# Mixture-of-experts output: accumulating scatters into a DRAM copy of the residual, in place of two scattered halves that are added on chip

## The chip, the cores and the metric

One core of a Trainium2 chip runs the whole program once. The metric is the device time of one execution in microseconds (us), given as the median of several runs. A profile is one execution with its instructions and transfers recorded. The engines are named as the profile names them: PE (matrix multiply), PEld (its weight loads), DVE (vector), ACT (scalar), POOL (GpSimd), SP (the engine that issues most transfers).

## The reference, cut to what matters

Two layers over 512 tokens of 1024 float32 values. Layer 0 mixes tokens with a recurrence (RWKV-7), layer 1 with forgetting attention ("fox" in the code). Each mixer is followed by a mixture of 16 experts, two of which each token uses:

```python
for i in range(DEPTH):                       # DEPTH = 2
    h = layer_norm(ALPHA * h + mixed, ln_g[i, 0], ln_b[i, 0])
    ffn = shared_router_moe(h, ...)          # top 2 of 16 experts for each token
    h = layer_norm(ALPHA * h + ffn, ln_g[i, 1], ln_b[i, 1])

# in shared_router_moe: gate = gate / sum(gate) for the two chosen experts, rows sorted by expert,
hid = silu(xb @ w_gate[e]) * (xb @ w_up[e]); ys = hid @ w_down[e]
out = segment_sum(ys * row_gate, row_tok)    # each token gets the sum of its two experts' rows
```

## The kernel before, in words

Tokens lie on 128 partitions, so 512 tokens are four token tiles (0 to 3). Matmuls are done in split precision: every weight and every input is split into a high and a low part (ACT copies the high part, DVE subtracts it), and three products are summed (lines 67 to 70). TensorE therefore runs three matmuls for one.

**Before an expert stage** each token tile is normalised (`ln_steps`), and `After.norm` (line 1300) writes it to the DRAM tensor `hd`: tiles 0 to 2 by POOL's queue, tile 3 by SP's.

**The expert stage** (`moe`) goes through the 16 experts in a fixed order. Weights come in pieces of 1 MB through eight buffers (`raw0` to `raw5`, `rawo0`, `rawo1`); a piece is asked for by SP when DVE has split what lay in its buffer (`wsplitB`). For expert e POOL issues, in this order: the scatter of expert e-1's rows (line 338), the gather of the rows of expert e+2 into `xg` (line 252), and the gather of the rows beyond 128 of expert e+1 into `xo` (line 261). PE turns `xo` in `xposeB` (line 309) near the end of expert e, between the two halves of its last weight piece, whether there are such rows or not. An expert with over 128 rows runs a further block `more(e)`, with a scatter of its own. The rows in one of two buffers `yt` are scattered with

```python
st=nc.gpsimd.indirect_dma_start(out=yd[:,:],out_offset=bass.IndirectOffsetOnAxis(ap=ix[0:n],axis=0),
    in_=y[0:n],in_offset=None,bounds_check=2*T-1,oob_is_err=False)
for o in scat: tc.declare_no_dep(st.ins,o.ins,reason="rows of other slots")
```

into a DRAM tensor `yd` of 1024 rows: row `token` for a token's first expert, row `512 + token` for its second (`dst`). No two scatters share a row, so none waits for another. Unused places in the list of 128 indices are out of bounds and are skipped.

**After the expert stage** `Combine` forms ALPHA*h + y0 + y1 for each token tile and normalises it. The last pieces of `load` bring `hd` back into `raw4` and `raw5` while the last expert runs. When all scatters have landed, SP issues eight loads from `yd` (line 474: y0 and y1 of four tiles). How a tile is summed is chosen by a letter: 'D' on DVE (line 493), 'G' on POOL and DVE (lines 487, 488), 'P' by matmuls with the identity into PSUM (line 482), 'V' partly so and the last addition on DVE (line 490). The layers use 'DVPG' and 'PVPV'. After layer 0, `fox` follows: each tile is normalised (lines 123 to 148), turned on PE (line 1075), split (lines 1076 and 1078), and the value matmuls start (line 68). After layer 1 the tiles are normalised and written out (line 1359). `spread` and `spread2` copy the norm's gain and bias to all partitions by way of PE and ACT.

The order of the work on each engine is written by `Threads.run`: generators give the planner their modelled durations, and it emits the steps in the order of modelled time. `FX_SCHED` holds the start times that it is given for the attention layer: four for the token tiles and one for the split of the value weights are its last numbers that matter here. `th.sooner` decides by the same model whether DVE or POOL does a multiplication or addition of the norm's gain and bias (line 148).

## Time and profile before

| what | value |
|---|---|
| median of 3 runs | 1652.01 us (1647.05 to 1655.39) |
| the profiled execution, its own time | 1651.01 us |
| its span, first to last instruction | 1649.3 us |
| PE / PEld / DVE / ACT / POOL busy | 90% / 73% / 71% / 56% / 31% |
| mean granted TensorE clock | 0.93 |
| transfers | 317.81 MB, 193 GB/s over the span |

The two expert stages lie at about 535 to 887 us and 1257 to 1608 us, the attention layer between them, and the last norm after 1608 us. A busy share is an average over stages with different limits, so the stages are read one by one below. The profiled execution lies 1.0 us under the median of the runs shown.

### The profile page before, as it was taken

To read this page: it belongs to the slowest core of one execution; us is meant where nothing else is said; L and a number is where in the kernel's file an instruction comes from. 1 tells how busy PE (TensorE), PEld (TensorE's weight loads), DVE (VectorE), ACT (ScalarE), POOL (GpSimd) and SP (SyncE) were. 2 spreads that over 40 slices of the span, in tenths; PEclk is the share of its full clock that TensorE was granted. 3 is DMA by queue.
4 is the path that set the end of the run, shared out by engine and by line. 5 is a ranking of instruction groups with operands and counts; after the bars stand their busy time and mean duration, and the time that the engine had idled before them with its cause. 6 is when DMAs were issued, how large, how long until landed. Compare 5 with 4: busy or idle time off the path is not lost. (4 is left out here: it accounts for less than half of the span.)

```text
span 1649.3 us, 25004 instructions
## 1 busy us (share of the span) xinstructions
PE 1485.4 (90%) x9185; PEld 1199.9 (73%) x9185; DVE 1173.0 (71%) x1883; ACT 924.3 (56%) x1359; POOL 519.3 (31%) x423
## 2 busy tenths in 40 slices
PE   6998976988885999999998799999985999999995
PEld 2587865877764788888885677777674888888882
DVE  7647779577685796968995637556647786969874
ACT  2554574534334585858784436545424876858753
POOL 4104775413331442333321422101105332323311
PEclk8989998688996999999998899999996999999997
DMA  7325532133435697988994223112417896969954
GB/s 219 122 83 192 161 101 72 27 100 113 131 119 207 225 360 262 331 299 296 363 321 173 92 72 121 46 51 71 163 68 237 268 365 235 365 232 359 352 179 156
DMA packets 203609, 317.81 MB, mean 193 GB/s; under 512 B 27978, under 2 KB 123554, under 8 KB 203444
## 3 DMA queue, kind: packets, MB, share of 16 engines
q1 hardware_dynamic: 181060, 276.13, 49.3%
q0 software_dynamic: 17664, 33.11, 5.8%
q10 hardware_dynamic: 4720, 6.44, 1.1%
q8 instruction: 94, 1.54, 0.4%
q14 instruction: 71, 0.58, 0.1%
HBM read 304.80 MB, written 37.55 MB: 208 GB/s over the span
## 5 line engine op out<-in xcount | busy, mean ns | idle before, releaser
L202 DVE TENSOR_TENSOR wl<-raw,wh 128x2048 fp32r<-128x2048 f32 (+1 forms) x168 | 334.5, 2005 | 5.6 <-DVEq L345 5.6
L199 ACT ACTIVATE wh<-raw 128x2048 fp32r<-128x2048 f32 (+1 forms) x168 | 282.6, 1688 | 14.1 <-ACT wh L199 8.6
L68 PE MATMUL bank<-wh,xm 128*128 128x256 f32 (+1 forms) x768 | 249.8, 325 | 3.9
L69 PE MATMUL bank<-wl,xm 128*128 128x256 f32 (+1 forms) x768 | 245.1, 319 | 0.0
L70 PE MATMUL bank<-wh,xm 128*128 128x256 f32 (+1 forms) x768 | 245.0, 319 | 0.0
L338 POOL DMA_INDIRECT yd<-yt,TB x38 | 91.4, 2406 | 438.2 <-ACT yt L305 389.7
L68 PEld LDWEIGHTS bank<-wh,xm 128*128 128x128 f32 x768 | 144.6, 188 | 26.1 <-issue 14.6
L69 PEld LDWEIGHTS bank<-wl,xm 128*128 128x128 f32 x768 | 144.7, 188 | 11.4
L70 PEld LDWEIGHTS bank<-wh,xm 128*128 128x128 f32 x768 | 144.5, 188 | 11.4
L202 DVE TENSOR_TENSOR wl<-rawo,wh 128x2048 fp32r<-128x2048 f32 (+1 forms) x56 | 110.2, 1980 | 24.9 <-ACT wh L199 24.4
L68 PE MATMUL bank<-wh,wh 128*128 128x512 f32 x256 | 112.4, 439 | 3.1 <-DVE wl L1078 1.7
L68 PE MATMUL bank<-wh,hm 128*128 128x512 f32 x256 | 111.3, 435 | 0.0
L70 PE MATMUL bank<-wh,wl 128*128 128x512 f32 x256 | 102.2, 399 | 2.6 <-DVE wl L1264 2.6
L69 PE MATMUL bank<-wl,wh 128*128 128x512 f32 x256 | 101.5, 396 | 0.0
L70 PE MATMUL bank<-wh,hm 128*128 128x512 f32 x256 | 101.0, 395 | 0.0
L69 PE MATMUL bank<-wl,hm 128*128 128x512 f32 x256 | 100.8, 394 | 0.0
L199 ACT ACTIVATE wh<-rawo 128x2048 fp32r<-128x2048 f32 (+1 forms) x56 | 93.4, 1669 | 12.8 <-PE bank L70 9.0
L1086 POOL TENSOR_TENSOR wl<-raw,wh 128x512 fp32r<-128x512 f32 x29 | 41.4, 1442 | 86.7 <-ACT wh L1085 86.7
L261 POOL DMA_INDIRECT xo<-hd,TB x30 | 62.2, 2072 | 13.0 <-issue 8.6
L64 ACT ACTIVATE xm<-bank 128x512 fp32r<-128x512 f32 x64 | 38.3, 598 | 46.4 <-PE bank L279 45.3
L68 PEld LDWEIGHTS bank<-wh,wh 128*128 128x128 f32 x256 | 49.4, 193 | 16.4 <-issue 5.7
L1221 ACT ACTIVATE sb<-sb,st 128x512 f32<-128x512 f32 (+1 forms) x64 | 35.7, 559 | 45.7 <-DVE st L1217 29.3
(544 smaller groups left out, 3561.4 us busy)
## 6 DMA issues: line engine op xcount, KB each, us to landing
raw<-in_moe_w_gate_dram SPq DMA_DIRECT2D x48, 1024.0 KB, 8.5
raw<-in_moe_w_up_dram SPq DMA_DIRECT2D x48, 1024.0 KB, 9.9
raw<-in_moe_w_down_dram SPq DMA_DIRECT2D x48, 1024.0 KB, 7.5
rawo<-in_moe_w_up_dram SPq DMA_DIRECT2D x16, 1024.0 KB, 5.5
rawo<-in_moe_w_down_dram SPq DMA_DIRECT2D x16, 1024.0 KB, 7.5
rawo<-in_moe_w_gate_dram SPq DMA_DIRECT2D x14, 1024.0 KB, 8.3
raw<-in_fx_w_in_dram SPq DMA_DIRECT2D x12, 1024.0 KB, 6.3
raw<-in_rw_wk_dram SPq DMA_DIRECT2D x4, 1024.0 KB, 12.5
```

Of the source, the lines that this page charges most:

```text
L64: nc.scalar.activation(hi,src,AF.Copy)
L68: nc.tensor.matmul(out,ah,bh,start=start,stop=False)
L69: nc.tensor.matmul(out,ah,bl,start=False,stop=False)
L70: nc.tensor.matmul(out,al,bh,start=False,stop=stop)
L199: Q=slice(None) if q is None else QS[q]; nc.scalar.activation(his[m%NH][:,Q],raws[m%NR][:,Q],AF.Copy)
L202: Q=slice(None) if q is None else QS[q]; V.tensor_tensor(los[m%NH][:,Q],raws[m%NR][:,Q],his[m%NH][:,Q].bitcast(F32),op=ALU.subtract)
L261: nc.gpsimd.indirect_dma_start(out=xo,out_offset=None,in_=hd.rearrange("t (h n) -> (t h) n",h=2), in_offset=bass.IndirectOffsetOnAxis(ap=T ...
L338: st=nc.gpsimd.indirect_dma_start(out=yd[:,:],out_offset=bass.IndirectOffsetOnAxis(ap=ix[0:n],axis=0), in_=y[0:n],in_offset=None,bounds_ch ...
L1086: (V if d else G).tensor_tensor(lo[n][:,Q],raw[:,Q],hi[n][:,Q].bitcast(F32),op=ALU.subtract)
L1221: S.activation(SB[u][:,0:N],SB[u][:,0:N],AF.Exp,bias=ST[u][:,0:1],scale=-1.0,accum_out=ST[u][:,1:2])
```

## The change

A second DRAM tensor, `zd`, gets a copy of each normalised tile beside `hd` (four more writes for each layer, all by POOL's queue). The expert rows are added into `zd` by the scatter itself (`compute_op=ALU.add`), at row `token` (`src`), for a token's first and second expert alike. The declaration that scatters are independent is gone, so each scatter waits for the one before it to land. The gates are divided by ALPHA, so that `zd` ends as h + ffn/ALPHA, and the norm's epsilon is divided by ALPHA squared. `Combine` loses its letters, its additions, its loads of `hd` and `yd`; it loads four tiles of `zd`. The start times of the attention layer's token tiles go from 2, 5, 8, 11 to 0, 2, 4, 6 and that of the value weights' split from 20 to 15; the last norm's tiles start 2 modelled us apart instead of 3.

```diff
-    nc.vector.tensor_scalar(sm[:,14:15],sm[:,13:14],LN_EPS,None,op0=ALU.add)
+    nc.vector.tensor_scalar(sm[:,14:15],sm[:,13:14],eps,None,op0=ALU.add)
...
-        scat=[]
         def scatter(ix,y,n):
-            st=nc.gpsimd.indirect_dma_start(out=yd[:,:],out_offset=bass.IndirectOffsetOnAxis(ap=ix[0:n],axis=0),
-                in_=y[0:n],in_offset=None,bounds_check=2*T-1,oob_is_err=False)
-            for o in scat: tc.declare_no_dep(st.ins,o.ins,reason="rows of other slots")
-            scat.append(st)
+
+            nc.gpsimd.indirect_dma_start(out=zd[:,:],out_offset=bass.IndirectOffsetOnAxis(ap=ix[0:n],axis=0),
+                in_=y[0:n],in_offset=None,bounds_check=T-1,oob_is_err=False,compute_op=ALU.add)
...
-                scatter(dst(e,1),y,64)
+                scatter(src(e,1),y,64)
...
-            lo(4); dnA(w[5],5,1); outA(1,y,fo); scatter(dst(e),y,128); hi(5); lo(5)
+            lo(4); dnA(w[5],5,1); outA(1,y,fo); scatter(src(e),y,128); hi(5); lo(5)
...
-        V.tensor_tensor(red[:,2,0:4],red[:,1,0:4],red[:,1,4:8],op=ALU.add); V.reciprocal(red[:,2,0:4],red[:,2,0:4])
+        V.tensor_tensor(red[:,2,0:4],red[:,1,0:4],red[:,1,4:8],op=ALU.add); V.reciprocal(red[:,2,0:4],red[:,2,0:4]); V.tensor_scalar(red[:,2,0:4],red[:,2,0:4],1.0/ALPHA,None,op0=ALU.mult)
...
-    def load_h(s, j):
-        s.C.nc.sync.dma_start(s.C.raws[4+j].rearrange("p (i n) -> p i n",i=2),s.hd[j*256:(j+1)*256,:].rearrange("(i p) n -> p i n",p=128))
-    def load_y(s, yd, y1, late):
...
-    def add(s, i, t, **k):
-        for n in range(2): s.C.nc.tensor.matmul(s.C.bk[2*i+n],s.C.ident,t[:,n*512:(n+1)*512],skip_group_check=True,**k)
+    def load_z(s):
+        for i in range(NT): s.C.nc.sync.dma_start(s.h[i],s.zd[i*128:(i+1)*128,:])
...
-        yield from ln_steps(C,th,z,i,s.h[i],s.gb,s.bb)
+        yield from ln_steps(s.C,th,s.h[i],i,s.h[i],s.gb,s.bb,eps=LN_EPS/ALPHA**2)
...
-FX_SCHED=(0,.5,-1,0,2,5,8,11,20)+(0,)*16
+FX_SCHED=(0,.5,-1,0,0,2,4,6,15)+(0,)*16
...
-    comb.load_y(yd,[tp.tile([128,D],F32,name=f"y1{i}") for i in range(NT)],True)
+    comb.load_z(); comb.spread(); comb.spread2()
...
         (s.C.nc.sync if i==NT-1 else s.C.nc.gpsimd).dma_start(s.hd[i*128:(i+1)*128,:],out)
+        s.C.nc.gpsimd.dma_start(s.zd[i*128:(i+1)*128,:],out)
...
-        cb[0].how='DVPG'
...
-        cb[1].how='PVPV'; cb[1].load_y(yd,[part(C.raws[i//2],i%2) for i in range(NT)],False)
+        cb[1].load_z()
         th=Threads()
         def last(i):
-            yield 3.0*i
+            yield 2.0*i
```

What moves is seen in the order of the instructions on an engine. At the start of the attention layer, PE has before the identity matmuls that sum the residual (line 482), then the turns of the tiles (line 1075), each row of which is one bank, and the first value matmul (line 68); `raw4` holds tiles 0 and 1, `raw5` tiles 2 and 3:

```order
L482 MATMUL bank2_3948<-raw4_65,ident_74 128x512 [waits DMAHW1_49,Activation_49]
L482 MATMUL bank3_3949<-raw4_65,ident_74 128x512
L482 MATMUL bank4_3950<-raw5_66,ident_74 128x512 [waits DMAHW2_49,Activation_49]
...
L1075 MATMUL bank0_3946<-ident_74,raw4_65 128x128 [waits DVE_49]
...
L1075 MATMUL bank1_3947<-ident_74,raw4_65 128x128 [waits DVE_49]
...
L1075 MATMUL bank2_3948<-ident_74,raw4_65 128x128 x4
L1075 MATMUL bank4_3950<-ident_74,raw5_66 128x128 [waits Activation_49,Pool_49]
...
L68 MATMUL bank0_3946<-wh0_3931,wh4_3935 128x512 [waits DVE_49]
```

Now the same stretch of PE has no sums, and the turns of six half tiles instead of four stand ahead of the first value matmul:

```order
L1051 MATMUL bank0_3952<-ident_74,raw4_65 128x128 [waits DMAHW1_49,DVE_49]
...
L1051 MATMUL bank1_3953<-ident_74,raw4_65 128x128 [waits Pool_49]
...
L1051 MATMUL bank2_3954<-ident_74,raw4_65 128x128 [waits DMAHW2_49,Pool_49]
...
L1051 MATMUL bank3_3955<-ident_74,raw4_65 128x128 [waits DVE_49]
...
L1051 MATMUL bank4_3956<-ident_74,raw5_66 128x128 [waits DMAHW3_49,DVE_49,Activation_49]
...
L1051 MATMUL bank6_3958<-ident_74,raw5_66 128x128 [waits DMAHW4_49,Activation_49,Pool_49]
...
L68 MATMUL bank0_3952<-wh0_3937,wh4_3941 128x512 [waits Activation_49]
```

The first value matmul has thus moved behind the turns of the first halves of tiles 2 and 3 (`bank4`, `bank6`).

At the very end, DVE before takes the statistics of tile 0 from PSUM (`bank0`, `bank1`) when PE has summed it, and adds for tile 1 (line 490) ahead of its statistics:

```order
L123 BN_STATS sm_90<-bank0_3946 128x6 [waits PE_49]
L123 BN_STATS sm_90<-bank1_3947 128x6 [waits PE_49]
L124 BN_AGGR sm_90<-sm_90 128x2 [waits DVE_49]
...
L148 TENSOR_TENSOR raw4_65<-raw4_65,raw2_63 128x512 [waits DMAHW2_49,DMAHW0_49,Activation_49]
L490 TENSOR_TENSOR raw4_65<-raw0_61,bank2_3948 128x512 [waits DMAHW7_49,PE_49]
L490 TENSOR_TENSOR raw4_65<-raw0_61,bank3_3949 128x512 [waits PE_49]
```

Now its statistics wait for a load alone:

```order
L123 BN_STATS sm_90<-raw4_65 128x6 [waits DMAHW4_49]
L123 BN_STATS sm_90<-raw4_65 128x6
L124 BN_AGGR sm_90<-sm_90 128x2 [waits DVE_49]
...
L123 BN_STATS sm_90<-raw4_65 128x6 [waits DMAHW5_49]
...
L148 TENSOR_TENSOR raw4_65<-raw4_65,raw2_63 128x512 [waits DMAHW3_49,Pool_49]
L123 BN_STATS sm_90<-raw5_66 128x6 [waits DMAHW6_49]
```

PE has left this chain, and no addition stands between the statistics of one tile and the next.

In the expert stage, POOL before issues the two gathers and the scatter of one expert, with `xg` and `xo` the gathered rows and `yt` the rows to be scattered; the scatter waits for ACT, which writes its rows, and for the transfer that last used its buffer:

```order
L338 DMA yd0_3960<-yt1_3971,TB_3962 1024x1024 [waits DMASW0_49,DVE_49]
L345 UNCONDITIONAL_BRANCH
L345 ISA [waits DMASW0_49]
...
L252 DMA xg0_3968<-hd0_135,TB_3962 128x1024 [waits DMASW1_49,PE_49]
L261 DMA xo_3972<-hd0_135,TB2_3963 128x512 [waits DVE_49,DMASW6_49,PE_49,Activation_49]
L338 DMA yd0_3960<-yt0_3970,TB_3962 1024x1024 [waits DMASW3_49,Activation_49]
```

Now:

```order
L339 DMA zd0_137<-yt1_3976,TB_3967 512x1024 [waits DMASW3_49,DVE_49]
L344 UNCONDITIONAL_BRANCH
L344 ISA [waits DMASW4_49]
...
L253 DMA xg0_3973<-hd0_135,TB_3967 128x1024 [waits DMASW5_49,PE_49]
L262 DMA xo_3977<-hd0_135,TB2_3968 128x512 [waits DVE_49,DMASW2_49,PE_49,Activation_49]
L339 DMA zd0_137<-yt0_3975,TB_3967 512x1024 [waits DMASW4_49,DMASW3_49,Activation_49]
```

The order on POOL is the same; the last row has one more wait, for the scatter before it (`DMASW4`).

## Rows read from the trace of the kernel before

**Rows 1.** Busy time of each engine in one regular expert: us, busy (instructions), clock, DMA, GB/s.

```profile
794.90:813.87 18.97, 18.82 (x113) 16.26 (x112) 17.20 (x16) 15.34 (x17) 6.91 (x3) 1.00 1.03 361
```

**Rows 2.** Timeline of POOL in that expert: start, us, instruction, [idle before <- releaser].

```profile
794.90 2.81 POOL L338 DMA_INDIRECT yd<-yt,TB  x1 [11.45 <-ACT yt L305]
798.01 1.88 POOL L252 DMA_INDIRECT xg<-hd,TB  x1 [0.30 <-issue]
800.20 2.22 POOL L261 DMA_INDIRECT xo<-hd,TB  x1 [0.31 <-issue]
```

**Rows 3.** Transfers issued in that expert: last number, us from issue to landing.

```profile
yd<-yt,TB POOLq DMA_INDIRECT x1, 9.1
xg<-hd,TB POOLq DMA_INDIRECT x1, 8.8
xo<-hd,TB POOLq DMA_INDIRECT x1, 7.4
```

**Rows 4.** Timeline of PE in that expert: the turn of `xo`.

```profile
810.03 0.60 PE L309 MATMUL bank<-ident,xo 128*128 128x128 f32 x4
```

**Rows 5.** Timelines of POOL and DVE around an expert with a further block.

```profile
633.29 2.80 POOL L338 DMA_INDIRECT yd<-yt,TB  x1 [11.45 <-ACT yt L305]
...
645.96 0.68 DVE L335 TENSOR_TENSOR yt<-xo,bank 64x512 f32<-64x512 f32 x1 [2.93 <-ACT xo L335]
```

**Rows 6.** Timeline of all engines at the start of the attention layer.

```profile
887.67 1.00 POOL L338 DMA_INDIRECT yd<-yt,TB  x1 [14.06 <-ACT yt L305]
...
893.50 0.35 SPq L474 DMA_DIRECT2D rawo<-yd  x1
...
897.11 1.22 DVE L493 SCALAR_TENSOR_TENSOR raw<-raw,rawo 128x1024 f32<-128x1024 f32 x1 [13.68 <-DMA rawo<-yd]
...
902.43 1.29 DVE L123 BATCH_NORM_STATS2 sm<-raw 128x6 f32<-128x512 f32 x2
...
903.75 0.21 DVE L124 BATCH_NORM_AGGREGATE sm<-sm 128x2 f32<-128x12 f32 x1
...
904.18 0.20 ACT L126 ACTIVATE sm<-sm 128x1 f32<-128x1 f32 x1 [4.79 <-DVE sm L125]
...
905.59 0.15 DVE L130 RECIPROCAL sm<-sm 128x1 f32<-128x1 f32 x1
...
907.71 1.50 ACT L135 ACTIVATE raw<-raw,sm 128x512 f32<-128x512 f32 x2
...
908.59 1.26 POOL L148 TENSOR_TENSOR raw<-raw,raw 128x512 f32<-128x512 f32 x1 [13.87 <-ACT raw L135]
...
913.09 1.12 PE L1075 MATMUL bank<-ident,raw 128*128 128x128 f32 x4 [4.41 <-DVE raw L148]
...
921.25 0.68 DVE L1078 TENSOR_TENSOR wl<-bank,wh 128x512 fp32r<-128x512 f32 x1
...
921.98 0.79 PE L68 MATMUL bank<-wh,wh 128*128 128x512 f32 x1 [1.66 <-DVE wl L1078]
```

**Rows 7.** Busy time of each engine after that (columns as in rows 1).

```profile
922.00:927.00 5.00, 5.00 (x18) 4.07 (x19) 4.47 (x11) 3.41 (x7) 0.68 (x1) 0.62 0.00 0
```

**Rows 8.** Timeline of all engines at the end of the program.

```profile
1614.22 0.34 SPq L474 DMA_DIRECT2D rawo<-yd  x1
...
1625.33 0.70 DVE L123 BATCH_NORM_STATS2 sm<-bank 128x6 f32<-128x512 f32 x1 [20.32 <-PE bank L482]
...
1632.30 0.69 DVE L148 TENSOR_TENSOR raw<-raw,raw 128x512 f32<-128x512 f32 x1
...
1641.50 4.07 DVE L148 TENSOR_TENSOR raw<-raw,raw 128x512 f32<-128x512 f32 x6
```

**Rows 9.** All transfers issued by line 474, from issue to landing.

```profile
DMA to landing us min/median/max: 3.5/7.9/10.5
```

**Rows 10.** Timelines of POOL and SP ahead of the first expert stage.

```profile
498.50 0.54 POOL L1303 DMA_DIRECT2D hd<-res  x1 [6.50 <-DVE res L148]
...
517.02 0.58 POOL L192 MEMSET TB<- 128x256 int32 x2 [17.99 <-PE rb L159]
```

More of the change, by code (lines that the diff above doesn't have):

```diff
@@ L138, in ln_affine, with ln_steps @@
     C.nc.vector.tensor_tensor(z,z,gb,op=ALU.mult); eng.tensor_tensor(z,z,bb,op=ALU.add)
-def ln_steps(C, th, z, i, out, gb, bb, mark=lambda n: None):
-    ln_stats(C,z,i); yield 'V',1.4,'S',.2,.1
+def ln_steps(C, th, z, i, out, gb, bb, mark=lambda n: None, eps=LN_EPS):
+    ln_stats(C,z,i,eps); yield 'V',1.4,'S',.2,.1
     ln_scale(C,i); yield 'V',.2,.1
@@ L175, in place, with moe @@
     queue.dma_start(raw.rearrange("p (k n) -> p k n",k=kk),(M[:,hf*n:(hf+1)*n] if w==1 else M[hf*128*kk:(hf+1)*128*kk,:]).rearrange("(k p) n -> p k n",p=128))
-def moe(C, L, W, hd, load, tail, late=()):
+def moe(C, L, W, hd, zd, load, tail, late=()):
     nc,tc=C.nc,C.tc; V=nc.vector
@@ L446, in moe, with __init__ @@
                     with tc.If(rs[e]>max(192,128*blk)): rest(e,blk)
-    return yd
 class Combine:
-    def __init__(s, C, hd, g, b):
-        s.C,s.hd,s.g,s.b=C,hd,g,b; s.how='PPPP'
-        s.h=[part(C.raws[4+i//2],i%2) for i in range(NT)]; s.y0=[part(C.raws[6+i//2],i%2) for i in range(NT)]
+    def __init__(s, C, zd, g, b):
+        s.C,s.zd,s.g,s.b=C,zd,g,b
+        s.h=[part(C.raws[4+i//2],i%2) for i in range(NT)]
         s.gb,s.bb=part(C.raws[2],0),part(C.raws[2],1)
@@ L1038, in fox_vload, with fox @@
     C.nc.sync.dma_start(k4(dst),P['win'][k*512:(k+1)*512,2048+n*512:2048+(n+1)*512].rearrange("(k p) n -> p k n",p=128))
-FX_SCHED=(0,.5,-1,0,2,5,8,11,20)+(0,)*16
-def fox(C, comb, yd, P, after):
+FX_SCHED=(0,.5,-1,0,0,2,4,6,15)+(0,)*16
+def fox(C, comb, P, after):
     nc,tc=C.nc,C.tc
@@ L1295, with __init__ @@
 class After:
-    def __init__(s, C, hd, load, gb, bb):
-        s.C,s.hd,s.load,s.gb,s.bb=C,hd,load,gb,bb
+    def __init__(s, C, hd, zd, load, gb, bb):
+        s.C,s.hd,s.zd,s.load,s.gb,s.bb=C,hd,zd,load,gb,bb
     def free(s, n): s.load(n)
@@ L1314, with __init__ @@
 class AfterFox(After):
-    def __init__(s, C, hd, load, lg, lb):
-        After.__init__(s,C,hd,load,part(C.raws[2],0),part(C.raws[2],1)); s.lg,s.lb=lg,lb
+    def __init__(s, C, hd, zd, load, lg, lb):
+        After.__init__(s,C,hd,zd,load,part(C.raws[2],0),part(C.raws[2],1)); s.lg,s.lb=lg,lb
     def free(s, n):
@@ L1330, in trunk @@
         nc.scalar.dma_start(C.rwt,a["router_w"].rearrange("(k p) e -> p k e",p=128)); nc.scalar.dma_start(C.rbt,bcast_row(a["router_bias"]))
-        hd=[C.dram.tile([T,D],F32,name=f"hd{n}") for n in range(2)]
+        hd,zd=[[C.dram.tile([T,D],F32,name=f"{c}d{n}") for n in range(2)] for c in "hz"]
         lg=lambda n: (a["ln_g"][n//2,n%2],a["ln_b"][n//2,n%2])
@@ L1340, in tail0 @@
             if k==3: cb[0].load_gb1()
-            if k in (4,5): cb[0].load_h(k-4)
         def tail1(k):
             if k==2: cb[1].load_gb()
-            if k in (4,5): cb[1].load_h(k-4)
         load=[loader(C,0,W,tail0),loader(C,1,W,tail1)]
         ctx.enter_context(tc.manual_schedule())
-        rwkv(C,a["x"][0],P,lambda gb,bb: After(C,hd[0],load[0],gb,bb),*lg(0))
+        rwkv(C,a["x"][0],P,lambda gb,bb: After(C,hd[0],zd[0],load[0],gb,bb),*lg(0))
         mk_ring(C)
-        cb=[Combine(C,hd[n],*lg(2*n+1)) for n in range(2)]
-        yd=moe(C,0,W,hd[0],load[0],2,(6,7))
-        cb[0].how='DVPG'
-        fox(C,cb[0],yd,F,AfterFox(C,hd[1],load[1],*lg(2)))
-        yd=moe(C,1,W,hd[1],load[1],0)
-        cb[1].how='PVPV'; cb[1].load_y(yd,[part(C.raws[i//2],i%2) for i in range(NT)],False)
+        cb=[Combine(C,zd[n],*lg(2*n+1)) for n in range(2)]
+        moe(C,0,W,hd[0],zd[0],load[0],2,(6,7))
+        fox(C,cb[0],F,AfterFox(C,hd[1],zd[1],load[1],*lg(2)))
+        moe(C,1,W,hd[1],zd[1],load[1],0)
+        cb[1].load_z()
         th=Threads()
         def last(i):
-            yield 3.0*i
+            yield 2.0*i
             yield from cb[1].steps(i,th)
```

26 lines of the change are left out of this document (4 added, 22 removed).

## The prediction

> **What bounds the kernel now.** I read the busy time by stage first. In a regular expert, the stretch between one expert's scatter and the next, TensorE works 18.82 of 18.97 us at full granted clock, while the transfers keep 361 GB/s up and the share of busy transfer engines is 1.03 [rows 1]. So TensorE bounds the expert stage, with the transfers close behind. 24 experts, 12 in each layer, repeat this pattern with 18.9 to 19.0 us each. The scatters move nothing there that TensorE waits for directly: what is on offer lies outside the expert stage, in the two places where TensorE has nothing to do because the residual is being summed and normalised.
>
> The first is the start of the attention layer. The last scatter is issued at 887.67, the first load of the sums at 893.50, and the first value matmul runs at 921.98 [rows 6]: 28.5 us, in which the reader sees DVE sum (897.11, 1.22 us each), take statistics (902.43), ACT normalise (907.71), POOL or DVE add the bias, PE turn (913.09), DVE split (921.25). After it PE is busy 5.00 of 5.00 us, at a granted clock of 0.62 at first [rows 7]. So whatever starts it earlier is kept, unless a later input is missing.
>
> The second is the end. The loads start at 1614.22, the first statistics at 1625.33, 11.1 us later; the row of the last six DVE operations starts at 1641.50 and fills 4.07 us [rows 8], to 1645.57, and the span ends at 1649.3 by the page. That is 35.1 us from first load to end, with no TensorE work behind it to hide anything.
>
> **The change, part by part.**
>
> *Fewer loads.* Four tiles of 512 KB are loaded where eight were. Loads of this line land 3.5 us (fastest), 7.9 (median), 10.5 (slowest) after issue [rows 9]; the fast ones were the first ones, with little queued before them: at the attention start the first sum begins 897.11 - 893.50 = 3.6 us after the first issue [rows 6]. With half the bytes I take 4.5 for the first tile that matters, the others following every 1 to 2 us, faster than DVE uses them; bounds 3.5 and 7.9.
>
> *Start of the attention layer.* Removed: the sums on DVE (1.22 each [rows 6]), the sums on PE with ACT's scaling, and the wait for the second half of each. What is left is one chain on DVE. In the new order DVE has, up to the first value matmul, four tiles' statistics (4 x 1.29 = 5.2), the aggregations and small operations (0.21 and 0.15 each, 3.0 in all), five multiplications or additions by line 148 (0.69 each [rows 8], 3.5), one split (0.68), about 0.3 of waits: 12.7, with the durations of [rows 6]. Behind the first tile's DVE work stand one POOL addition of 1.26 and turns of 1.12 [rows 6], so the chain is 15.1; I take 15.5, since ACT's normalisations (1.50 for a tile) now come two modelled us apart and can queue. 4.5 + 15.5 = 20.0 us from first load to first value matmul, against 28.5: **-8.5**. That the first value matmul now stands behind the turns of halves of all four tiles is inside this: those turns wait for the fourth tile's normalisation, which the 12.7 includes.
>
> *End.* 4.5 for the load; DVE then has statistics 5.2, sixteen small operations 3.2, eleven halves by line 148 at 0.69 = 7.6, in all 16.0; the tail from the last DVE operation to the end stays at 1649.3 - 1645.57 = 3.7. Sum 24.2 against 35.1: **-10.9**.
>
> *The accumulating scatter itself.* No row of before shows a transfer that adds. The nearest are the plain scatter (2.81 us on POOL, or 1.00 when DVE is quiet, as at 887.67; landing 9.1 after issue) and the gathers (8.8 and 7.4) [rows 2, 3, 6]. It has to read the row that it adds to, so I expect it to land later; from 0 later to as long again as the last scatter took to the first load, 893.50 - 887.67 = 5.83. I take +2.0 at each layer's end, nearer to nothing since 64 rows on average are little beside the weights: **+4.0**, bounds 0 and +11.7.
>
> *Waits of a scatter on the one before.* Behind a waiting scatter on POOL stand the gathers of `xg` and `xo` of the next expert, and PE waits for `xo`. But scatters are 18.97 us apart and land after 9.1 [rows 1, 3], so the wait is over 9.9 us before it is met. Cost nothing, with that cover; without it, see the rivals. In experts with a further block the distance is shorter, and there the same buffer `yt` is written again 645.96 - 633.29 = 12.7 us after its scatter was issued [rows 5]: 3.6 us of cover.
>
> The Trainium skill, page "DMA: Bandwidth & Descriptors", section "Rules for kernel authors", asks for this wait: an accumulating transfer reads its destination and writes it later, and another write in between is lost, so one must wait for the earlier one's semaphore. By that rule the scatters can't be let go again, and the cover of 9.9 us is all there is; no run here has shown it yet.
>
> *The second copy.* Four more writes per layer on POOL's queue, 0.54 us each [rows 10], after each tile's norm. They stand before POOL's 17.99 us of idle time ahead of line 192 [rows 10], which hides 4 x 0.54 = 2.2 us, and before the first gather only by that. Bounds 0 and 3 (all of it, and a later buffer, since the piece that follows the third tile into its buffer has one more reader); I take 0.5 per layer: **+1.0**. One DVE operation for the gates, 0.15 in each layer [rows 6], on the path to the first gather: **+0.3**. The changed constants of the norm cost nothing. The loads of `hd` fall away from the last expert, 4 MB less in all; TensorE bounds there, so nothing is gained.
>
> *Sum.* -8.5 - 10.9 + 4.0 + 1.0 + 0.3 = -14.1 against the profiled execution's own 1651.0: 1636.9. That execution lies 1.0 us under the median, so **1638**. With all bounds at their good end (loads 3.5 twice: -2.0; scatters at 0: -4.0; copies at 0: -1.0) it is 1631; with all at the bad end (+6.8, +7.7, +5.0) 1657. That is the likeliest case's own range.
>
> **The rivals.**
>
> *xo comes late (slower).* The accumulating scatter is issued ahead of both gathers on the same POOL queue. `xo` is issued at 800.20 and lands 7.4 later, at 807.6; PE turns it at 810.03 [rows 2 to 4]: 2.4 us of slack, 2.4 to 2.8 over the regular experts. If the adding scatter takes longer on POOL, or its reads and writes hold the queue ahead of the gathers, the delay beyond 2.4 us falls on PE in each of 24 experts. The gain of 14.1 is eaten at 2.4 + 14.1/24 = 3.0 us of delay: it decides from there. At 4.4, half of the plain scatter's landing of 9.1 put in front of the gathers [rows 3], 24 x 2.0 = 48 us come on top, 1686; at the far bound, a whole 9.1, 24 x 6.7 = 161. For it: the transfers' share of 1.03 [rows 1] leaves little room, and POOL's 2.81 us for a scatter against 1.00 at 887.67 shows that its issue is touchy [rows 2, 6]. Against: the gathers issued right behind the plain scatter land within 9 us although that one is still in flight, so transfers of this queue overlap.
>
> *The adding scatter lands after 15 us or more (slower).* Its rows then hold `yt` in the experts with a further block: six blocks in the two layers, each with 12.7 us until the buffer is written [rows 5]. A landing of 18.2, twice the 9.1, would cost up to 6 x 5.5 = 33 us, and some 3 more at each layer's end than I took: about 1677. It decides from 12.7 + 14.1/6 = 15.0 us. Beyond 18.97 every expert would wait, at some 30 us for each us. For it: nothing in the rows, only that the transfer reads twice. Against: the added bytes are few, 64 rows of 4 KB for an expert against 6.9 MB in the stretch of rows 1.
>
> The Trainium skill, page "Collectives: The Full Stack", section "The bandwidth ceiling: the fold count and why AG ≠ RS ≠ AR", has the reduction run at half the rate of the copy because each piece needs two reads, with a read descriptor for each. By that rule this rival's 18.2 would be met; no row of before tells.
>
> *The start of attention gives nothing back (no change).* If a later input (a weight piece, the split of the value weights moved from 20 to 15, the fox gates) holds PE after 922, the -8.5 goes and -10.9 + 4.0 + 1.3 = -5.6 is left: 1646. For it: the order of five modelled starts was moved at once. Against: PE without a gap in rows 7.
>
> *The change does less than it says:* the four letters removed had the sums partly on PE and POOL beside DVE's own work; if DVE alone was the limit before as well, only its 1.22 us sums go (some 5 us at each place, against 8.5 and 10.9). -10 + 5.3 gives 1647, the same side as the last one; its chance is in that one's.
>
> **How the numbers follow.** Forecast 0.61, `xo` late 0.14, landing late 0.08, no gain at the attention start (or a smaller one) 0.17. About 0.5%, 8 us, is what a measurement of this kernel can tell from no change. The bound for faster is thus 1644: most of the forecast's case lies under it; its bad end and the third rival lie between 1644 and 1660, but a part of the third rival (loads at their good end) is faster too. Slower by over 8 us means 1660 and more: the first two rivals. So faster 0.62, same 0.16, slower 0.22. The range goes from 1628 (a little under the forecast's good end, for a chain on DVE shorter than 15.5) to 1664: what is left out is most of the two slower rivals, and little below.
>
> **What would show it.** In the changed kernel's profile: first load to first value matmul 20 us (28.5 before); first load to the end of the span 24 us (35.1); landing of scatters 10 to 13 us; regular experts still 18.97 us, with no wait of PE on `xo` at its turn. A scatter row on POOL well over 2.8 us, or PE idle ahead of line 310 with `xo` as releaser, shows the first rival; DVE idle on `yt` or POOL idle on a scatter ahead of line 339 the second; PE gaps shortly after the first value matmul the third. The forecast is wrong if the expert stage grows at all: 0.6 us for each regular expert is the whole gain.

## The result, and the profile after

The changed kernel takes 1634.19 us (median of 4 runs, 1633.03 to 1635.95), the kernel before 1650.8 beside it: ratio 0.9899, 95% interval 0.9871 to 0.9927, or 16.6 us less. 1638 was predicted, 1628 to 1664 as range. The profiled execution took 1635.95 us with a span of 1634.2, 15.1 us under the span of before.

To see where they went, cut both spans at the same instructions. Each number is the distance between the starts of two rows of the timeline; the last column adds up to the difference of the spans.

| from, to | before | after | difference |
|---|---|---|---|
| start, first write of `hd` (recurrence) | 476.5 | 478.8 | +2.4 |
| to the first scatter of layer 0 | 82.6 | 83.6 | +1.0 |
| to the last scatter (16 experts) | 328.6 | 328.4 | -0.2 |
| to the first load | 5.8 | 6.9 | +1.0 |
| to the first value matmul | 28.5 | 20.0 | -8.5 |
| to the first write of `hd` of layer 1 | 271.7 | 268.7 | -3.0 |
| to the first scatter of layer 1 | 86.9 | 87.1 | +0.3 |
| to the last scatter | 328.7 | 329.4 | +0.7 |
| to the first load | 5.0 | 6.4 | +1.4 |
| to the end | 35.1 | 24.9 | -10.2 |

The first place is the start of the attention layer. The timeline of after, to be held against [rows 6] (start, us, engine, line, operation, idle time before and what ended it):

```profile
890.84 1.60 POOL L339 DMA_INDIRECT zd<-yt,TB  x1 [13.65 <-ACT yt L306]
...
897.69 1.78 SPq L467 DMA_DIRECT2D raw<-zd  x4
...
901.05 1.29 DVE L123 BATCH_NORM_STATS2 sm<-raw 128x6 f32<-128x512 f32 x2 [14.63 <-DMA raw<-zd]
...
905.63 1.74 DVE L148 TENSOR_TENSOR raw<-raw,raw 128x512 f32<-128x512 f32 x1
...
907.43 2.24 PE L1051 MATMUL bank<-ident,raw 128*128 128x128 f32 x8 [8.83 <-DVE raw L148]
...
912.97 1.57 DVE L148 TENSOR_TENSOR raw<-raw,raw 128x512 f32<-128x512 f32 x1
...
914.59 3.45 PE L1051 MATMUL bank<-ident,raw 128*128 128x128 f32 x12 [2.48 <-DVE raw L148]
...
915.22 1.65 POOL L148 TENSOR_TENSOR raw<-raw,raw 128x512 f32<-128x512 f32 x1 [1.23 <-DVE raw L148]
...
917.70 0.72 PE L68 MATMUL bank<-wh,wh 128*128 128x512 f32 x1
```

No sum stands ahead of the statistics any more: they start 3.4 us after the first load, where the first ones of before started 8.9 us after it. The turns (line 1051) follow the additions by line 148, and the value matmul follows the turns.

The second place is the end, to be held against [rows 8]:

```profile
1602.91 1.58 POOL L339 DMA_INDIRECT zd<-yt,TB  x1 [13.46 <-ACT yt L306]
...
1609.27 1.77 SPq L467 DMA_DIRECT2D raw<-zd  x4
1612.88 1.28 DVE L123 BATCH_NORM_STATS2 sm<-raw 128x6 f32<-128x512 f32 x2 [14.19 <-DMA raw<-zd]
...
1616.16 4.16 POOL L148 TENSOR_TENSOR raw<-raw,raw 128x512 f32<-128x512 f32 x3 [11.67 <-ACT raw L135]
...
1617.46 1.74 DVE L148 TENSOR_TENSOR raw<-raw,raw 128x512 f32<-128x512 f32 x1
...
1623.62 6.70 DVE L148 TENSOR_TENSOR raw<-raw,raw 128x512 f32<-128x512 f32 x9
```

The statistics start 3.6 us after the first load (11.1 before), DVE then works to 1630.32 without a gap worth naming, and 3.9 us later the span ends. One multiplication by line 148, beside POOL's additions of the same line, took 1.74 instead of 0.69.

What held the first statistics back in the kernel before was less a load than PE. It first multiplied the scaled `hd` rows of all four tiles by the identity, in 10.04 us, and took the first loaded rows at 1622.56, 8.3 us after the first load was issued, without a wait for them. Timeline of PE before, and busy time in that stretch, with a granted clock of 0.69:

```profile
1612.52 10.20 PE L482 MATMUL bank<-raw,ident 128*128 128x512 f32 x16 [4.20 <-ACT raw L477]
1622.56 1.88 PE L482 MATMUL bank<-rawo,ident 128*128 128x512 f32 x4
```

```profile
1612.52:1622.56 10.04, 10.04 (x17) 4.27 (x18) 0.00 (x0) 4.06 (x4) 0.00 (x0) 0.69 0.74 270
```

The expert stage is as it was. One regular expert of after, busy time of each engine (us, then busy time and, in brackets, instructions of PE, PEld, DVE, ACT and POOL; then clock, share of busy transfer engines, GB/s), and the timeline of POOL with PE's turn of `xo`; [rows 1 to 4] are the same of before:

```profile
688.59:707.56 18.97, 18.82 (x113) 16.26 (x112) 17.13 (x16) 15.37 (x17) 6.92 (x4) 1.00 1.05 368
```

```profile
688.59 3.40 POOL L339 DMA_INDIRECT zd<-yt,TB  x1 [11.46 <-ACT yt L306]
692.29 1.30 POOL L253 DMA_INDIRECT xg<-hd,TB  x1 [0.30 <-issue]
693.90 2.22 POOL L262 DMA_INDIRECT xo<-hd,TB  x1 [0.31 <-issue]
...
703.71 0.60 PE L310 MATMUL bank<-ident,xo 128*128 128x128 f32 x4
```

The same 18.97 us and 18.82 us of PE. The adding scatter holds POOL 3.40 us instead of 2.81, but the gather behind it 1.30 instead of 1.88, so `xo` is issued 5.31 us after the scatter where it was 5.30.

### The profile page after: what moved, and what is told of

Its sections match the earlier page's. It is cut to its first block, busy times and chain, and to the rows that moved or that the text cites. A ratio compares the mean times of both kernels' runs of the same rounds, so it can differ in the third digit from the quotient of the medians.

```text
span 1634.2 us, 24892 instructions
## 1 busy us (share of the span) xinstructions
PE 1459.5 (89%) x9125; PEld 1192.7 (73%) x9125; DVE 1163.1 (71%) x1873; ACT 919.5 (56%) x1355; POOL 530.7 (32%) x431
## 5 line engine op out<-in xcount | busy, mean ns | idle before, releaser
L339 POOL DMA_INDIRECT zd<-yt,TB x38 | 113.7, 2992 | 432.2 <-ACT yt L306 386.0
L203 DVE TENSOR_TENSOR wl<-rawo,wh 128x2048 fp32r<-128x2048 f32 (+1 forms) x56 | 110.2, 1980 | 24.9 <-ACT wh L200 24.4
L262 POOL DMA_INDIRECT xo<-hd,TB x30 | 61.1, 2037 | 11.9 <-issue 8.6
L68 PEld LDWEIGHTS bank<-wh,wh 128*128 128x128 f32 x256 | 49.2, 192 | 15.1 <-issue 6.0
```

The costliest lines, as they stand in the source:

```text
L68: nc.tensor.matmul(out,ah,bh,start=start,stop=False)
L203: Q=slice(None) if q is None else QS[q]; V.tensor_tensor(los[m%NH][:,Q],raws[m%NR][:,Q],his[m%NH][:,Q].bitcast(F32),op=ALU.subtract)
L262: nc.gpsimd.indirect_dma_start(out=xo,out_offset=None,in_=hd.rearrange("t (h n) -> (t h) n",h=2), in_offset=bass.IndirectOffsetOnAxis(ap=T ...
L339: nc.gpsimd.indirect_dma_start(out=zd[:,:],out_offset=bass.IndirectOffsetOnAxis(ap=ix[0:n],axis=0), in_=y[0:n],in_offset=None,bounds_check ...
```

## The experiments

Two theories stood at the start of the experiments. By the first, the gain is what the prediction said: two chains on DVE that became shorter, with the adding scatters costing a little at each layer's end and nothing among the experts. By the second, the new start times carry it, or half the bytes to load. All stages of the profiled execution of each run, cut as above (us; "change" is the changed kernel):

| kernel | first hd | to scatter | experts 0 | to load | to value matmul | to hd | to scatter | experts 1 | to load | to end |
|---|---|---|---|---|---|---|---|---|---|---|
| before | 476.5 | 82.6 | 328.6 | 5.8 | 28.5 | 271.7 | 86.9 | 328.7 | 5.0 | 35.1 |
| change | 478.8 | 83.6 | 328.4 | 6.9 | 20.0 | 268.7 | 87.1 | 329.4 | 6.4 | 24.9 |
| e1_plain | 479.5 | 83.9 | 329.2 | 6.0 | 20.2 | 269.9 | 87.6 | 313.8 | 5.1 | 24.9 |
| e2_own_rows | 483.6 | 84.3 | 328.8 | 5.6 | 20.5 | 270.2 | 87.6 | 313.8 | 5.2 | 25.1 |
| e3_before_copies | 480.0 | 83.8 | 329.3 | 5.8 | 29.0 | 271.8 | 89.0 | 327.0 | 5.6 | 34.6 |
| e4_old_times | 471.8 | 83.4 | 328.7 | 6.5 | 19.6 | 276.6 | 87.1 | 329.5 | 6.4 | 25.1 |
| e5_before_new_times | 474.5 | 84.3 | 328.5 | 5.8 | 34.1 | 278.8 | 87.2 | 328.5 | 5.2 | 34.2 |
| e6_old_split | 478.0 | 84.4 | 328.7 | 6.4 | 23.2 | 276.8 | 87.5 | 329.2 | 6.7 | 24.9 |
| e7_hold_2 | 473.6 | 84.1 | 331.2 | 6.6 | 20.1 | 270.5 | 87.7 | 332.0 | 6.6 | 24.8 |
| e8_hold_6 | 476.4 | 84.5 | 353.8 | 6.6 | 20.0 | 270.4 | 87.6 | 352.5 | 6.4 | 25.0 |
| e9_probe | 479.0 | 84.4 | 328.5 | 8.1 | 19.9 | 270.4 | 88.0 | 327.7 | 6.6 | 24.9 |
| e10_late_landing | 477.6 | 83.7 | 332.5 | 6.1 | 20.0 | 270.5 | 87.3 | 336.1 | 6.3 | 24.8 |
| e11_eight_loads | 474.7 | 83.3 | 328.7 | 7.3 | 20.4 | 270.5 | 87.5 | 328.4 | 6.5 | 25.0 |
| e12_end_pe | 482.0 | 84.3 | 328.9 | 6.6 | 20.0 | 269.5 | 87.4 | 329.3 | 6.4 | 27.1 |

The first column is the same code in all of them and goes from 471.8 to 483.6. Totals that differ by a few us therefore say little here; the stages say more.

**The addition.**

```diff
-                in_=y[0:n],in_offset=None,bounds_check=T-1,oob_is_err=False,compute_op=ALU.add)
+                in_=y[0:n],in_offset=None,bounds_check=T-1,oob_is_err=False)
```

> The changed kernel with a plain scatter in place of the adding one: the rows overwrite zd, so the addition (residual, second expert) is left out; rows, waits, loads and order are the same. Theory: the addition itself costs only what the two layer ends showed, 1.0 and 1.4 us from last scatter to first load, plus 0.6 us of POOL's time for a scatter, which a shorter gather issue makes up: last scatter to first load falls from 6.85 to about 5.8 us at the attention start and from 6.4 to about 5.0 at the end, expert stages stay within 0.5 us of 328.4 and 329.4, total 2 to 3 us under the changed kernel (about 1632). Rival (adding burdens the expert stage too, by its second read): the expert stages become shorter as well, by more than 1 us each.

Median 1622.1 us, ratio to before 0.9819 (0.9783 to 0.9855). The total can't be compared: without the sums, layer 1 routes other tokens, its expert stage takes 313.8 us and has one scatter fewer. Last scatter to first load fell by 0.8 (6.9 to 6.0) and 1.3 (6.4 to 5.1), as expected, and the experts of layer 0 did not become shorter. Over all profiles this distance is 5.0 to 6.0 us with plain scatters and 6.1 to 7.3 with adding ones (8.1 in e9). POOL in a regular expert is back at the times of before:

```profile
690.49 2.81 POOL L339 DMA_INDIRECT zd<-yt,TB  x1 [11.45 <-ACT yt L306]
693.60 1.88 POOL L253 DMA_INDIRECT xg<-hd,TB  x1 [0.30 <-issue]
```

So the 3.40 and the 1.30 both come with the addition, and the expert stage does not show either.

**The wait of a scatter for the one before.**

```diff
+        scat=[]
         def scatter(ix,y,n):
-            nc.gpsimd.indirect_dma_start(out=zd[:,:], ... compute_op=ALU.add)
+            st=nc.gpsimd.indirect_dma_start(out=yd[:,:], ...)
+            for o in scat: tc.declare_no_dep(st.ins,o.ins,reason="rows of other slots")
+            scat.append(st)
```

> The changed kernel with the scatter of the kernel before: into a tensor of 1024 rows, with no waits among scatters, and the four loads read 512 of those rows; the sum of residual and expert rows is left out. What it takes away beside e1 is the wait of each scatter for the one before. Theory: that wait is always met before it is reached, so the time is that of e1 within 1 us. Rival (waits of scatters cost something, above all in experts with a further block, where scatters stand 14.5 us apart): it is faster than e1, by up to 1 us for each of the six such experts.

Median 1619.83 (ratio 0.9796, 0.976 to 0.9832; again with another layer 1, the same as that of e1, 313.8 us in both). Experts of layer 0: 328.8 against 329.2 of e1. The waits cost nothing that these stages show. These are plain scatters; that the adding ones don't wait for each other either is read from the changed kernel's profile, where the one before ends the wait of none of the 38 scatters (ACT or DVE, which write its rows, end it, as ACT does in the rows above).

**When it lands.**

```diff
             if e+1<NE: gather2(e+1)
+            if e>1: nc.gpsimd.dma_start(probe,zd[0:1,0:128])
             expert(e)
```

> The changed kernel with a small load (128 values of one row of zd) on POOL's queue behind the gathers of each expert from the third on; it waits for the scatter before it, so its start tells when the adding scatter has landed. POOL has nothing else to do there until the next scatter. Theory: landing 9 to 13 us after the scatter's issue (9.1 for the plain one before), so the wait of the next scatter, 18.97 us later, is met, and the time stays that of the changed kernel. Rival (second read makes it twice as long): 15 to 18 us, close to the next scatter.

1639.35 us in one run. The start of the probe, a little load that waits for the scatter, tells when the scatter has landed at the latest. The timeline of POOL:

```profile
689.94 3.44 POOL L339 DMA_INDIRECT zd<-yt,TB  x1 [6.98 <-ACT yt L306]
...
700.99 0.55 POOL L439 DMA_DIRECT2D probe<-zd  x1 [3.52 <-DMA zd<-yt,TB]
...
708.91 3.45 POOL L339 DMA_INDIRECT zd<-yt,TB  x1 [7.38 <-ACT yt L306]
```

It starts 11.0 us after the scatter's issue. Over the whole run the 22 probes behind a scatter and a gather came after 9.6 to 12.1 us; the plain scatters of the kernel before landed after 7.2 to 10.5 there, the one of [rows 3] after 9.1. Eight us are left until the next scatter. The scatters that no gather follows landed earlier. For the one ahead of the last expert the probe came after 6.7 and 6.6 us in the two layers (plain 4.8 and 4.9). For the last scatter of all, both kernels' profiles have the landing itself (last number, us from issue to landing; before, then after):

```profile
yd<-yt,TB POOLq DMA_INDIRECT x1, 3.1
...
zd<-yt,TB POOLq DMA_INDIRECT x1, 4.6
```

So without gathers behind it an adding scatter landed 1.5 us later than a plain one, or at most 1.9 by the probes.

**A later landing.**

```diff
             with tc.If(rs[e]>128):
+                if e: scatter(src(e-1),ys[(e-1)%2],128)
```

> The changed kernel with the scatter of the expert before issued a second time at the head of each further block (its rows are then added twice, so the sums are not the reference's; layer 1 then routes other tokens and only layer 0 can be compared). The second scatter waits for the first to land and holds the buffer yt until it has landed itself. Theory: the first lands after 9 to 13 us, the second as long after its own issue, 18 to 26 us after the first issue, and DVE, which writes yt 12.7 us after it in such a block, waits 5 to 13 us in each of the two such experts of layer 0; layer 0's expert stage grows from 328.4 us by 10 to 26. Rival: landing is 5 us or less, the wait of DVE is under 1 us and the stage stays.

1646.84 us in one run. Four more scatters ran, two in each layer, and the timeline of one shows the chain that the second rival described:

```profile
634.94 3.40 POOL L339 DMA_INDIRECT zd<-yt,TB  x1 [11.47 <-ACT yt L306]
646.06 1.57 POOL L339 DMA_INDIRECT zd<-yt,TB  x1 [7.72 <-DMA zd<-yt,TB]
...
653.40 0.68 DVE L336 TENSOR_TENSOR yt<-xo,bank 64x512 f32<-64x512 f32 x1 [8.70 <-DMA zd<-yt,TB]
```

DVE waited 8.70 us, against 2.93 before [rows 5], until `yt` was free, 18.5 us after its first scatter was issued. Over the four blocks DVE waited 30.0 us, 7.5 each, so 4.6 us more than the 2.9 that it waits anyway; the two expert stages grew by 4.1 and 6.7 us. The waits of DVE are as long as expected, but the stage of layer 0 grew by 4.1 and not by 10 to 26. The rival's mechanism exists, at 2.7 us for a block whose buffer is late by 4.6 (2.0 if layer 0 alone is counted, the one that the expectation lets count), and in four blocks rather than six: ahead of the first expert of a layer no scatter is in flight.

**The slack of `xo`.** Six and 22 small memsets stand between a scatter and the gathers:

```diff
             more(e)
+            if e>1:
+                for _ in range(6): nc.gpsimd.memset(hold,0.0)
```

> The changed kernel with six small memsets on POOL (about 1.7 us in all) between a scatter and the next gathers, for all experts from the third on. Theory (slack of 2.4 us at the turn of xo, as read from the kernel before, where xo is issued 5.30 us after the scatter as it is now, 5.31): a regular expert stays at 18.97 us. Rival (the slack is already used up by the adding scatter): each regular expert grows by about the held time beyond what is left, 0.5 us or more.

> As the last one with 22 memsets, about 6 us. Theory: PE waits at the turn of xo for the held time less 2.4 us, so a regular expert takes 18.97 + 3.6 to 4 us, for some 20 experts 70 to 85 us in all; experts with a further block less, since their gathers stand further from the turn. Rival (the weights' slack or a later turn absorbs it): under 1 us for each expert.

1638.84 and 1684.86 us, one run each. With six, `xo` was issued 2.5 us later (7.85 after the scatter), more than the 1.7 meant, and the expert stages grew by 2.8 and 2.7 us: the edge of the slack. PE waited in 9 of the experts, 0.6 us each. The gather of one and the turn that it released, in the timeline:

```profile
712.21 2.78 POOL L262 DMA_INDIRECT xo<-hd,TB  x1 [0.31 <-issue]
...
720.14 0.42 PEld L310 LDWEIGHTS bank<-ident,xo 128*128 128x128 f32 x4 [0.93 <-DMA xo<-hd,TB]
720.15 0.65 PE L310 MATMUL bank<-ident,xo 128*128 128x128 f32 x4 [0.49 <-DMA xo<-hd,TB]
```

With 22 it was issued 11.9 us after the scatter, 6.6 later than in the changed kernel, and PE waited in nearly every held expert, in the same view:

```profile
685.21 1.01 POOL L262 DMA_INDIRECT xo<-hd,TB  x1 [0.31 <-DMA zd<-yt,TB]
691.37 0.42 PEld L310 LDWEIGHTS bank<-ident,xo 128*128 128x128 f32 x4 [2.25 <-DMA xo<-hd,TB]
691.37 0.66 PE L310 MATMUL bank<-ident,xo 128*128 128x128 f32 x4 [1.81 <-DMA xo<-hd,TB]
...
694.34 3.16 POOL L339 DMA_INDIRECT zd<-yt,TB  x1 [8.12 <-ACT yt L306]
```

25.4 and 23.1 us on the two expert stages, about 24 for 13 held experts, 1.9 us each, half of the 3.6 to 4 expected. The slack of 2.4 us is confirmed: PE begins to wait where the issue is 2.5 us later. The price beyond it was set too high, and two rows of the held expert say why. The gather that is issued later also lands sooner, 6.2 us after issue here (691.37 - 685.21), with 1.01 us on POOL, where it took 7.4 and 2.22 [rows 2, 3]. And the next scatter follows the turn after 2.97 us (694.34 - 691.37), where it took 3.85 in the changed kernel (703.71 to 707.56). Together these are 2.1 of the 2.3 us that are missing from 4.2 (6.6 - 2.4).

**The copies.** The kernel before with the writes added:

```diff
         (s.C.nc.sync if i==NT-1 else s.C.nc.gpsimd).dma_start(s.hd[i*128:(i+1)*128,:],out)
+        s.C.nc.gpsimd.dma_start(s.C.zd[s.hd.name if 0 else id(s.hd)][i*128:(i+1)*128,:],out)
```

> The kernel before with the four further writes of each layer on POOL's queue added, into a tensor that nobody reads; all else as before. Theory (as predicted): +0.5 us per layer, at most 1 us per layer, seen between the first write of hd and the first scatter (82.6 us before in layer 0, 83.6 in the changed kernel; 86.9 and 87.1 in layer 1). Rival: the writes cost the 1.0 us that layer 0 lost and more, 2 to 3 us in all, since the tables and first gathers share the queue with 2 MB more. The recurrence ahead of it, 2.4 us longer in the changed kernel's profile up to the first write of hd, is not touched by either kernel's code: theory says it varies from execution to execution and is not a part of the change.

1653.81 us, ratio 1.0011 (0.9989 to 1.0033). The way from `hd` to the first scatter became 83.8 and 89.0 us, 1.2 and 2.1 more than in the profile of before. But e5, which has no copies, shows 84.3 in layer 0: this stretch varies by as much without them. In layer 1, where the kernels without copies gave 86.9 and 87.2, the changed kernel and its variants gave 87.1 to 88.0. So the copies cost about 1 us for a layer at most in the changed kernel, and the 2.1 of e3 in layer 1, which its rival had (2 to 3 us in all), stands alone; more can't be told.

**The start times.** The changed kernel with the old ones, with the old one for the split of the value weights alone, and the kernel before with the new ones:

```diff
-FX_SCHED=(0,.5,-1,0,0,2,4,6,15)+(0,)*16
+FX_SCHED=(0,.5,-1,0,2,5,8,11,20)+(0,)*16
...
-            yield 2.0*i
+            yield 3.0*i
```

> The changed kernel with the start times of before for the token tiles (2, 5, 8, 11 and 20 in the attention layer, 3 us apart at the end). Theory: the gain comes from the sums and loads that are gone, the start times matter little: first load to first value matmul 20 to 22 us (20.0 changed, 28.5 before), first load to end 25 to 27 us (24.9 and 35.1), total 0 to 4 us over the changed kernel. Rival: the new start times carry it: first value matmul 24 us or later after the first load, end 29 us or more, so that at least half of the 8.5 and 10.2 us is gone; the further 2.9 us that the attention layer gained after its first value matmul is also gone.

> The changed kernel with one number of the start times put back, that of the value weights' split (20 in place of 15); the four tiles keep 0, 2, 4, 6. The stretch from first load to the next layer's first write of hd was 288.7 us in the changed kernel and 296.1 with all five old. Theory: the four tiles' times set the order at the start, and the split's number matters by less than 2 us (287 to 291). Rival: the split's number carries the 7.4 us (294 to 297).

> The kernel before with the new start times alone (0, 2, 4, 6 and 15 in the attention layer, 2 us apart at the end); its sums and eight loads stay. In the changed kernel the old times cost 7.4 us of the 11.9 that the stretch from the first load to the next layer's first write of hd gained, so one theory has the start times as the larger part of the gain: then this kernel's stretch falls from 300.1 us by 5 to 7 us (293 to 295). The other has the times useful only because the sums are gone (DVE reaches the tiles later here, so the order it is given does not match): then the stretch stays within 2 us of 300.1 or grows. The end stays at 35 us for both, since 3 or 2 us made no difference there in the changed kernel.

1640.45 us (ratio to before 0.9946, 0.992 to 0.9973), 1647.41 (one run) and 1664.22 (ratio 1.0087, 1.0062 to 1.0113). The old times thus cost 6.3 us in all, where up to 4 were expected. The end did not move by more than 0.9 us in any. The attention layer did: from first load to the next write of `hd`, the sum of two columns, before has 300.1 us, the change 288.7 (288.7 to 290.9 over the nine runs with this code), old times 296.1, the old split alone 300.0 (in one execution; more than all five old numbers together, which neither expectation had), and the kernel before with new times 312.8. So neither theory holds as written. The new times alone make the kernel before 12.7 us slower in this layer; the smaller chain with the old times saves 4.0; both together save about 10. And in e4 the first value matmul came earliest of all (19.6 us) with the layer still 7.4 us longer. Where it is lost is later. What PE waited for after its first value matmul comes to 10.7 us in e4 and to 7.3 in the changed kernel, so to 3.4 of the 7.4. The longest three of e4 (engine, line, waited for: us in total, times, longest):

```profile
PE bank L68 <- ACT wh L1239: 2.7, 2, 2.1
PE bank L68 <- DVE qs L1160: 2.7, 1, 2.7
PE bank L1183 <- DVE st L1193: 1.8, 2, 1.6
```

and the longest of the changed kernel:

```profile
PE bank L70 <- DVE wl L1240: 3.6, 2, 2.2
```

PE's busy time in e6 in two stretches, the second with a granted clock of 0.66:

```profile
977.50:997.50 20.00, 17.42 (x75) 13.68 (x73) 13.66 (x18) 11.87 (x21) 6.87 (x7) 0.91 0.47 146
...
1157.50:1177.50 20.00, 16.07 (x65) 11.49 (x66) 14.37 (x32) 12.11 (x29) 6.86 (x5) 0.66 0.47 158
```

In the changed kernel the first of them, at the same distance from the first load, is full. The second is not the same work there, since e6 runs later by then: near the end of its layer the changed kernel has a gap too, one stretch earlier, and at a higher clock.

```profile
977.70:997.70 20.00, 20.00 (x101) 15.75 (x100) 15.33 (x32) 13.19 (x26) 6.13 (x5) 1.00 0.40 125
...
1137.70:1157.70 20.00, 15.99 (x85) 10.74 (x84) 13.42 (x27) 12.69 (x27) 5.88 (x4) 0.99 0.16 53
1157.70:1177.70 20.00, 19.31 (x107) 14.60 (x108) 12.03 (x42) 7.26 (x22) 0.00 (x0) 0.93 0.47 159
```

The five numbers do not only start the tiles; they set the modelled times by which the planner orders the rest of the layer. That this order is the cause is argued from the gaps and not shown; which of its pieces costs what was not taken apart.

**The loads.**

```diff
         for i in range(NT):
-            s.C.nc.sync.dma_start(s.h[i],s.zd[i*128:(i+1)*128,:])
+            s.C.nc.sync.dma_start(s.h[i],s.zd[i*128:(i+1)*128,:]); s.C.nc.sync.dma_start(part(s.C.raws[6+i//2],i%2),s.zd[i*128:(i+1)*128,:])
```

> The changed kernel with each load of a zd tile followed by a second load of the same tile into a buffer that nobody reads, so that eight loads of 512 KB stand in the queue as before. Theory: of the 15.1 us less at the two places, the loads carry little, since DVE is the chain: statistics of the first tile start 3.4 to 4.5 us after the first load at both places (3.4 and 3.6 changed), the later tiles come before DVE needs them, the end stays at 25 to 26.5 us. Rival (half the bytes are the gain): the second to fourth tiles come 3 to 4 us apart, DVE waits for them, and the end grows by 5 us or more, to 30.

1634.14 us in one run; 20.4 us to the first value matmul, 25.0 at the end. The timeline at the end shows the second tile barely waited for:

```profile
1607.36 0.34 SPq L468 DMA_DIRECT2D raw<-zd  x1
...
1611.00 1.29 DVE L123 BATCH_NORM_STATS2 sm<-raw 128x6 f32<-128x512 f32 x2 [14.38 <-DMA raw<-zd]
1613.61 1.29 DVE L123 BATCH_NORM_STATS2 sm<-raw 128x6 f32<-128x512 f32 x2 [0.27 <-DMA raw<-zd]
```

Half the bytes are worth 0.4 and 0.1 us. At the same start times, those of before, the two places still go from 28.5 to 19.6 and from 35.1 to 25.1 us (e4). So the gain at both places is that of the sums, with the wait for each sum's second half: in e11 nothing waits for the further loads.

**Another end.** DVE bounds the end, so the bias was moved to PE and ACT:

```diff
+        Z=cb[1]
+        for i in range(NT):
+            for n in range(2): nc.tensor.matmul(C.bk[2*i+n],C.ident,Z.bb[:,n*512:(n+1)*512],start=True,stop=False,skip_group_check=True)
...
+                nc.vector.tensor_tensor(h[:,N],h[:,N],Z.gb[:,N],op=ALU.mult); yield 'V',.6
+                nc.tensor.matmul(bk,C.ident,h[:,N],start=False,stop=True,skip_group_check=True); yield 'P',.5
+                nc.scalar.activation(h[:,N],bk,AF.Copy); yield 'S',.6
```

> The changed kernel with the last norm's bias added by PE and taken out of PSUM by ACT (the bias rows are put into PSUM by matmuls with the identity before the loads land, the scaled tile is added by another), all multiplications by the gain on DVE; all else as changed. Theory (DVE sets the end): DVE loses four additions by line 148 and the slowing that POOL's additions bring to it (1.74 us for a multiplication beside POOL's, 0.69 alone), some 3.5 us of 17.4; PE and ACT add about 1.2 behind the last multiplication: the end falls from 24.9 to 22.5 us, the total to about 1632. Rival (transfers or ACT set the end): the end stays at 24.9 or grows.

Median 1639.08 (ratio 0.9916, 0.9888 to 0.9943), end 27.1 us: 2.2 longer, not 2.4 shorter. DVE did finish earlier, 18.3 us after the first load instead of 21.1; PE took its place. Busy time at the end of e12:

```profile
1624.50:1629.50 5.00, 2.05 (x3) 1.02 (x4) 4.56 (x13) 3.71 (x7) 0.00 (x0) 0.50 0.00 0
1629.50:1634.50 5.00, 5.00 (x9) 2.06 (x8) 1.90 (x3) 3.48 (x6) 0.00 (x0) 0.62 0.25 105
```

PE worked 2.05 us of the first of these stretches, and its granted clock was 0.50 and then 0.62, so the lower of its two levels (1.2 GHz) for most of it: 9 instructions in 5 us, and ACT and the output behind them. No run that forms the whole sum was faster than the changed kernel (e11 is the same).

## Why the prediction was right, and where not

- **Start of the attention layer** (-8.5 forecast): -8.5 measured, 20.0 us as said. The mechanism is the one that was forecast: DVE works from 901.05 to 915.14 with hardly a gap, on four tiles' statistics, five pieces by line 148 and one split, and POOL's addition (915.22) and a turn end the chain. That the sum came out to the tenth is luck: the load took 3.4 rather than 4.5, the chain behind it 16.6 rather than 15.5. DVE's part took 14.1 and not 12.7: two of its five pieces by line 148 took 1.74 and 1.57 us beside POOL's of the same line, and not 0.69. That half the bytes carry the gain falls with e11, and the fourth rival (1.22 us sums alone, 5 us at each place) with the 8.5 and 10.2.
- **What is kept of it.** The step "whatever starts it earlier is kept" was too simple, in both directions. In the changed kernel the layer gained 3.0 us more after the first value matmul (1.2 to 2.2 in the other eight runs of this code), and what gave them stays open. PE's clock suggests itself: after the first value matmul it ran 27 instructions in 5 us at a granted 0.95, against 18 at 0.62 in [rows 7]:

```profile
912.70:917.70 5.00, 2.97 (x13) 2.20 (x13) 5.00 (x7) 4.21 (x7) 3.75 (x3) 0.50 0.25 83
917.70:922.70 5.00, 5.00 (x27) 4.01 (x26) 4.53 (x8) 3.35 (x7) 2.25 (x2) 0.95 0.29 68
```

  But the other eight runs of this code, with the same 2.96 to 2.97 us of work ahead, have 21 to 27 instructions there at 0.68 to 0.95, and their gain does not go with it: 1.2 us in e11 (21 at 0.68) and 1.2 in e10 (27 at 0.93). And e4 shows that the third rival (nothing given back) was close: with the old start times 5.7 of the 9.7 us that these nine runs gain in the layer (median) are gone again by its end. The prediction saw the times move and gave them no term; they are worth these 5.7 us here, and cost 12.7 while the sums stand (e5).
- **End** (-10.9): -10.2. The load took 3.6 instead of 4.5, DVE 17.4 instead of 16.0, of which 1.05 is the one multiplication that took 1.74 beside POOL; the tail 3.9 instead of 3.7. What the 11.1 us of before were made of, PE's sums, the prediction did not read; it did not need to, since all of them went.
- **The adding scatter** (+4.0, bounds 0 to 11.7): +1.0 and +1.4, by e1 0.8 and 1.3 of them the addition's. In all 1.6 less than forecast, and inside the bounds.
- **Waits of scatters, landing** (no cost): right. Landing 9.6 to 12.1 us behind which a gather follows (10 to 13 was said), and no scatter of the changed kernel waits for another. In the further blocks that leaves little of the 3.6 us of cover, and DVE's wait there is still the one of before.
- **`xo` late**: did not happen, for a reason that was not foreseen: the adding scatter does hold POOL 0.6 us longer, and the next gather makes up just that. The slack of 2.4 us was right; the price beyond it, 24 us for each us, was about twice what e8 shows (48.5 us for 4.2). Half of the plain landing of 9.1, which this rival took as 4.4, is 4.6; nothing else hangs on it.
- **Two reads, twice the time**: the rule of the Trainium skill, page "Collectives: The Full Stack", section "The bandwidth ceiling: the fold count and why AG ≠ RS ≠ AR", does not carry over to these scatters: 9.6 to 12.1 us against 7.2 to 10.5, not twice as long (e9). There the Trainium skill has it for a ring of three or more ranks. The second rival would have needed 15.
- **Copies, gates** (+1.3): the profile shows +1.3 in the two stretches, but e5 shows as much without copies. Right in size, not shown in cause; for the gates no run was made.
- **The sum.** -14.1 was forecast against the profiled execution, -15.1 measured there. In it are +2.4 of the recurrence, which the change doesn't touch, and -3.0 of the attention layer, of which the other runs bear out 1.2 to 2.2. These two nearly cancel, which is luck as well. One small slip: the same sixteen small operations of DVE are put at 3.0 us in one chain and at 3.2 in the other, and the durations that are quoted make 2.6 of them.

## What to carry to other kernels

A chain that stands alone between two stages was worth its full length here. Taking the sums out of it left what a count of the remaining instructions on its busiest engine said, to within 1.5 us (15.5 and 16.0 forecast, 16.6 and 17.4 measured); the bytes that it no longer loads gave next to nothing. Where a planner's start times move with a change, price them as an edit of their own and look for the effect at the end of the layer, not at its first matmul. Work moved to a PE that has had little to do is priced at the clock that it gets there (0.50 to 0.62 in e12), not at that of its busy stages.
